# Attention scores of two pairs of heads as one block on TensorE, with the second pair's softmax a slot later

## The chip, the cores and the metric

The kernel runs on one core of a Trainium2 chip. The metric is the device time of one execution in microseconds (us). Before the change it was 1363.72 us, the median of three runs (1363.05 to 1364.31).

## The reference

One block of a streaming encoder for 256 tokens of 2048 channels, all in float32: a normalised input is projected by one wide matrix, a recurrent branch and an attention branch run side by side, sigmoid gates merge them, an output projection and an MLP of 8192 channels follow. The change lies in the attention branch alone. It has 16 heads of 64 channels, and 256 tokens are 4 chunks of 64:

```python
s = jnp.einsum('bhnqd,bhnkd->bhnqk', qc, kb) * (Dh ** -0.5) + bias[:, None]
s = jnp.where(valid[:, None, :], s, -jnp.inf)
p = jax.nn.softmax(s, axis=-1)
o = jnp.einsum('bhnqk,bhnkd->bhnqd', p, vb)
```

For each head, scores are made of queries and keys, a bias by relative distance is added, a softmax over the keys follows, and the result weighs the values.

## The kernel before, in words

**The gemms.** TensorE (PE) works without a break on large matrix products in float32 accuracy. Each piece of weights arrives by DMA (`raw_...`), ScalarE (ACT) rounds it to a high part (`wh_...`, line 91) and VectorE (DVE) subtracts to get the low part (`wl_...`, line 92); TensorE then makes three matmuls of 512 columns (lines 141 to 143: activation's high by `wh`, high by `wl`, low by `wh`). `Unit` with `run` makes 256 rows by 1024 columns in four PSUM banks (`c11`, `c12`, `c21`, `c22`, in the profile `acc_<unit>c`). Half of the inner dimension goes through seven products of blocks A, B, C, D of the weights (names such as `p21B`: bank 21, block B), the other half through plain pieces (`r0_8`: columns' half 0, inner tiles 8 and 9). A product or a piece is an item of 12 matmuls, and needs two splits of 1024 columns (a product) or one (a piece). Banks get sums and differences in between: ACT copies a bank to `u_...` (line 872), DVE subtracts it from another (line 908, called "less" below). GpSimd (POOL) issues accumulating DMAs between raw blocks (line 925).

**Slots.** `run` calls `u.step` at eleven places, the slots 0 to 10. Slot 2 lies after products 11D and 12C, and then come r1_8, slot 3, product 21A, slot 4, r1_10, slot 5, product 21B, slot 6, r0_8, slot 7, r0_10, slot 8, product 21D, slot 9, r0_12, slot 10 and the rest. Attention is cut into four pieces of work (two pairs of heads each), and each is hung on the slots of one unit: `av`, `qk`, `ga0` and `ga2`, which run one after the other.

**Attention of a pair of heads.** `attn_pair` makes the scores of two heads in one tile `s` of two PSUM banks (pool `ps_sc`, one buffer), head 0 in rows 0 to 63 and head 1 in rows 64 to 127 of the array, each in a first span of 128 columns and a second of 256 (line 694). POOL loads the bias by two DMAs of 128 KB (line 698) and masks a corner by a memset (line 699); the tile `bias` has one buffer, so that the bias of the next pair can be fetched only when the adds of this one have read it. DVE adds it (line 705, one instruction for each span, both heads in one), takes the maxima (`mx`, line 707), ACT takes the exponentials with their sums (line 710), and DVE scales by the reciprocals (`rs`, lines 712 and 714). Later slots turn the result by transposes on TensorE into the two banks of `ps_tp` (`turn`, tile `tpp`, line 720), ACT copies them out (line 722), and `attn_values` multiplies by the values (line 736), into a bank of `ps_tp` too.

**What sets the order.** Each engine runs its instructions in the order in which they stand, and an instruction whose input is late holds up all behind it. That order is made when the program is built, by a scheduler with priorities: score matmuls and weight splits are put ahead (`high_priority`), the adds and the rest of the softmax have none and are put where the scheduler holds them to be ready.

Of the kernel before, what the change touches and what calls it, by code (L numbers as in the profile page):

```python
# [8 lines left out]
F32 = mybir.dt.float32  # L9
# [3 lines left out]
ALU = mybir.AluOpType  # L13
# [3 lines left out]
P = 128  # L17
T = 256
# [4 lines left out]
NC = 512  # L23
# [27 lines left out]
def tile_hybrid_block(  # L51
# [5 lines left out]
    nc = tc.nc  # L57
# [8 lines left out]
    ps_acc, ps_tp, ps_sm = [cm.__enter__() for cm in ps_cms]  # L66
# [21 lines left out]
    casts, marks, newest, low = [], [], [], []  # L88
# [68 lines left out]
    def later(*steps):  # L157
        behind.extend([n, f] for n, f in steps)
# [109 lines left out]
    steps = [1, 1] + [2] * (KD // 2 - 1)  # L268
# [11 lines left out]
    for kt, n in zip(starts, steps):  # L280
# [6 lines left out]
        with ExitStack() as es:  # L287
# [3 lines left out]
            for j in range(n):  # L291
                g, hi = wmix[:, kt + j:kt + j + 1], xT[c][:, a + j, 0, :]
# [331 lines left out]
    def scores(n, made, gap, first=None, between=()):  # L624

        sc = []
        steps = []

        def one(i):
            if not i:  # L630
                out, fs = hgrn_scores(n, made)
                sc.extend(out)
                steps.extend(fs)
            steps[i]()

# [27 lines left out]
    s2 = scores(2, a2[0], 4)  # L663
# [3 lines left out]
    s3 = scores(3, a3[0], 4)  # L667
# [14 lines left out]
    ps_sc = ps_cms[-1].__enter__()  # L682
    yb = []
    TOK = 11

    def attn_pair(g, pr, qT, kT):

        n = g * 4 + pr
        sc = ps_sc.tile([P, 2, NC], F32, name=f"s{g}{pr}", tag="sc")
        with tc.issue_after(newest[0].ins), tc.high_priority(offset=2000):  # L690
            for d, q, k in ((slice(0, P), slice(0, P), slice(0, P)), (slice(P, 3 * P), slice(P, T), slice(0, T))):
                for j in range(2):
                    r = slice(64 * j, 64 * j + 64)
                    nc.tensor.matmul(sc[:, j, d], qT[r, q], kT[r, k], start=True, stop=True)
        bias = bp.tile([P, 2, T], F32, name=f"bias{n}", tag="bias", bufs=1)
        for j in range(2):
            rb = rel_bias[2 * n + j]
            nc.gpsimd.dma_start(bias[:, j, :], bass.AP(tensor=rb.tensor, offset=rb.offset + P + 1, ap=[[1, P], [1, T]]))
        nc.gpsimd.memset(bias[0:CH, :, 0:CH], NEG)
        s = bp.tile([P, 2, 3 * P], F32, name=f"sb{n}", tag="s", bufs=2)  # L700
        spans = (slice(0, P), slice(P, 3 * P))
        mx = small.tile([P, 2, 2], F32, name=f"mx{n}", tag="mx")
        sums = small.tile([P, 2, 2], F32, name=f"sum{n}", tag="sums")
        for d in spans:
            nc.vector.tensor_tensor(s[:, :, d], sc[:, :, d], rev(bias[:, :, 0:d.stop - d.start]), op=ALU.add)
        for b, d in enumerate(spans):
            nc.vector.tensor_reduce(mx[:, b, :], s[:, :, d], axis=AX.X, op=ALU.max, negate=True)
        for b, d in enumerate(spans):
            for j in range(2):
                nc.scalar.activation(s[:, j, d], s[:, j, d], AF.Exp, bias=mx[:, b, j:j + 1], accum_out=sums[:, b, j:j + 1])  # L710
        rs = small.tile([P, 2, 2], F32, name=f"rs{n}", tag="rs")
        nc.vector.reciprocal(rs, sums)
        for b, d in enumerate(spans):
            nc.vector.tensor_tensor(s[:, :, d], s[:, :, d], bc(rs[:, b, :], 2, d.stop - d.start), op=ALU.mult)
# [376 lines left out]
    qkT = {}  # L1091
# [37 lines left out]
    for m in range(NM):  # L1129
        scaled("k0", rstd, m, acc_k[m])  # L1130
    x_sums[3]()
    yb += [new_act(f"yb{g}") for g in range(2)]
    (p0, t0, v0), (p1, t1, v1), (p2, t2, v2), (p3, t3, v3) = chunks
    alone(Unit(lambda: xT, lambda: Sx, w_in_n, C_AV, "av", values,
               steps=at_slots((0, turn_of("k0")), (2, p0[0]), (4, p0[1]), (7, t0[0], t0[1]), (9, t0[2], t0[3])))) 

    def qk_done(m, n, acc):
        scaled("qk"[n] + "1", (rstd8, rstd)[n], m, acc)

    alone(Unit(lambda: xT, lambda: Sx, w_in_t, C_AQ + NC, "qk", qk_done, apart=HG,  # L1140
               steps=at_slots((0, v0), (1, p1[0]), (3, p1[1]), (6, t1[0], t1[1]), (9, t1[2], t1[3]))))
# [145 lines left out]
    def h_out(m, n, acc):  # L1287
        t = token(f"h1_{n}_{m}")
        with tc.high_priority(offset=2000):
# [10 lines left out]
                  steps=(lambda: h_blocks(0)) if n0 else (lambda: turned(mT, 3, "m3", ga)), start=2 if n0 else 0) for n0 in (0, 2)]  # L1300
    fin = {}
    for qd in range(NQ):
# [92 lines left out]
        for n0 in (0, 2):  # L1395
# [3 lines left out]
                              start=3 if n0 else 0, tail=last and n0 == 2, five=n0 == 2 and not last))  # L1399
# [49 lines left out]
```

## Time and profile before

| what | value |
|---|---|
| median of three runs | 1363.72 us (1363.05 to 1364.31) |
| profiled execution | 1363.58 us, of it 1361.9 us span |
| granted TensorE clock | 0.998 |
| PE busy | 1350.3 us, 99% of the span |
| DVE busy | 1166.9 us, 86% |
| ACT busy | 970.7 us, 71% |
| POOL busy | 156.3 us, 11% |
| the attention's slots | from about 250 to about 425 us of the span |

The span goes from the first to the last profiled instruction, and 1.7 us of the execution lie around it. A busy PE says that matmuls follow each other, with ends that are modelled; short waits are better seen in the starts of its instructions. In rows of a timeline the first number is the start and the second the duration, in us from the span's start; `[0.55 <-POOL bias L699]` says that the engine sat idle for 0.55 us and what ended it.

### The profile page before, as it was taken

To read this page: it belongs to the slowest core of one execution; us is meant where nothing else is said; L and a number is where in the kernel's file an instruction comes from. 1 tells how busy PE (TensorE), PEld (TensorE's weight loads), DVE (VectorE), ACT (ScalarE), POOL (GpSimd) and SP (SyncE) were. 2 spreads that over 40 slices of the span, in tenths; PEclk is the share of its full clock that TensorE was granted. 3 is DMA by queue.
4 is the path that set the end of the run, shared out by engine and by line. 5 is a ranking of instruction groups with operands and counts; after the bars stand their busy time and mean duration, and the time that the engine had idled before them with its cause. 6 is when DMAs were issued, how large, how long until landed. Compare 5 with 4: busy or idle time off the path is not lost.

```text
span 1361.9 us, 19182 instructions
## 1 busy us (share of the span) xinstructions
PE 1350.3 (99%) x6753; PEld 1116.1 (82%) x6753; DVE 1166.9 (86%) x1406; ACT 970.7 (71%) x1299; POOL 156.3 (11%) x239
## 2 busy tenths in 40 slices
PE   9999999999999999999999999999999999999997
PEld 7888888878778888888888888888888888888886
DVE  6888977887888988798998889898889988899885
ACT  6877765776777666556778767787667876678764
POOL 3000000110110000110121011100121001110210
PEclk9999999999999999999999999999999999999999
DMA  9655557778885988869898889998899988999892
GB/s 347 228 185 157 176 181 264 217 211 258 247 225 171 307 276 246 262 153 325 286 278 264 244 254 263 281 306 225 245 281 275 301 222 238 294 292 274 260 279 97
DMA packets 132498, 336.92 MB, mean 247 GB/s; under 512 B 11296, under 2 KB 14624, under 8 KB 132016
## 3 DMA queue, kind: packets, MB, share of 16 engines
q1 hardware_dynamic: 110816, 266.11, 56.4%
q0 software_dynamic: 21296, 69.28, 26.2%
q8 instruction: 53, 0.87, 0.2%
q14 instruction: 45, 0.37, 0.1%
q10 hardware_dynamic: 288, 0.29, 0.1%
HBM read 271.67 MB, written 10.49 MB: 207 GB/s over the span
## 4 chain that ended last, share of the span: by engine, by line
PE 98%; DMA 1%; ACT 0%; DVE 0%; issue 0%; SPq 0%; POOL 0%; POOLq 0%; DVEq 0%
PE acc_hq L183 2%; PE acc_hf L183 2%; PE tp_u L110 1%; PE acc_hq L188 1%; PE acc_hg L143 1%; PE acc_hi L143 1%; PE acc_hg L141 1%; PE acc_hi L142 1%; PE acc_hg L142 1%; PE acc_ga2c L141 1%; PE acc_hi L141 1%; PE acc_hf L188 1%; PE acc_ga0c L141 1%; PE acc_avc L141 1%; PE acc_dn30c L141 1%; PE acc_wo2c L143 1%
## 5 line engine op out<-in xcount | busy, mean ns | idle before, releaser
L183 PE MATMUL acc_hq<-act_x,wh_hq 128*128 128x512 f32 x128 | 41.0, 399 | 1.5 <-ACT wh_hq L91 1.2
L183 PE MATMUL acc_hf<-act_x,wh_hf 128*128 128x512 f32 x128 | 40.6, 398 | 0.4 <-DVE wh_hf L91 0.4
L1339 POOL DMA_DIRECT2D hd<-y x24 | 24.7, 1041 | 45.8 <-ACT y L1338 45.4
L188 PEld LDWEIGHTS acc_hf<-act_x,wl_hf 128*128 128x128 f32 x128 | 23.4, 188 | 5.4
L188 PEld LDWEIGHTS acc_hq<-act_x,wl_hq 128*128 128x128 f32 x128 | 23.4, 188 | 5.3 <-DVE wl_hq L92 0.2
L141 PE MATMUL acc_hg<-wh_hg,act_x 128*128 128x512 f32 x64 | 25.1, 392 | 0.0
L141 PE MATMUL acc_hi<-wh_hi,act_x 128*128 128x512 f32 x64 | 25.0, 391 | 0.0
L143 PE MATMUL acc_hg<-wh_hg,act_x 128*128 128x512 f32 x64 | 24.9, 390 | 0.0
L143 PE MATMUL acc_hi<-wh_hi,act_x 128*128 128x512 f32 x64 | 24.9, 389 | 0.0
L142 PE MATMUL acc_hi<-wl_hi,act_x 128*128 128x512 f32 x64 | 24.9, 389 | 0.0
L142 PE MATMUL acc_hg<-wl_hg,act_x 128*128 128x512 f32 x64 | 24.9, 389 | 0.0
L92 DVE TENSOR_TENSOR wl_hq<-raw_hq,wh_hq 128x1024 fp32r<-128x1024 f32 (+2 forms) x21 | 20.1, 966 | 5.4 <-ACT wh_hq L91 5.4
L188 PE MATMUL acc_hq<-act_x,wl_hq 128*128 128x256 f32 x128 | 24.6, 279 | 0.0
L188 PE MATMUL acc_hf<-act_x,wl_hf 128*128 128x256 f32 x128 | 24.6, 279 | 0.0
L92 DVE TENSOR_TENSOR wl_hf<-raw_hf,wh_hf 128x512 fp32r<-128x512 f32 (+2 forms) x26 | 20.9, 811 | 4.1 <-ACT wh_hf L91 3.9
L91 ACT CAST wh_hq<-raw_hq 128x1024 fp32r<-128x1024 f32 (+2 forms) x21 | 17.6, 842 | 8.9 <-DMA raw_hq<-in_w_in_t_dram 4.6
L92 DVE TENSOR_TENSOR act_u<-tp_u,act_u 128x512 fp32r<-128x512 f32 x28 | 19.2, 685 | 5.3 <-ACT act_u L91 5.3
L100 POOL TENSOR_TENSOR ro<-os,mhalf 128x4 f32<-128x4 f32 x4 | 4.4, 1099 | 167.4 <-DVE os L99 164.3
L92 DVE TENSOR_TENSOR wl_hg<-raw_hg,wh_hg 128x1024 fp32r<-128x1024 f32 x16 | 19.4, 1219 | 3.0 <-ACT wh_hg L91 3.0
L183 PEld LDWEIGHTS acc_hq<-act_x,wh_hq 128*128 128x128 f32 x128 | 19.9, 189 | 2.2 <-ACT wh_hq L91 1.4
L183 PEld LDWEIGHTS acc_hf<-act_x,wh_hf 128*128 128x128 f32 x128 | 19.9, 190 | 1.0 <-DVE wh_hf L91 0.7
L91 ACT CAST wh_hf<-raw_hf 128x512 fp32r<-128x512 f32 (+2 forms) x24 | 17.5, 740 | 4.4 <-PE acc_hg L143 1.6
(2295 smaller groups left out, 5327.3 us busy)
## 6 DMA issues: line engine op xcount, KB each, us to landing
raw_hi<-in_w_in_n_dram SPq DMA_DIRECT2D x16, 512.0 KB, 3.8
raw_hg<-in_w_in_n_dram SPq DMA_DIRECT2D x16, 512.0 KB, 3.7
raw_hq<-in_w_in_t_dram SPq DMA_DIRECT2D x12, 512.0 KB, 5.2
hd<-y POOLq DMA_DIRECT2D x24, 256.0 KB, 8.6
raw_hf<-in_w_in_t_dram SPq DMA_DIRECT2D x16, 256.0 KB, 5.6
raw_hf<-in_w_in_t_dram SPq DMA_DIRECT2D x8, 512.0 KB, 4.0
raw_aq<-in_w_in_t_dram SPq DMA_DIRECT2D x8, 512.0 KB, 4.4
raw_ak<-in_w_in_t_dram SPq DMA_DIRECT2D x8, 512.0 KB, 4.3
```

Source lines behind the costliest of these rows:

```text
L91: casts[:] = [(copy or nc.scalar.copy)(hi, src)]
L92: low[:] = [nc.vector.tensor_tensor(lo, src, hi.bitcast(F32), op=ALU.subtract)]
L100: nc.gpsimd.tensor_tensor(dst, ms, mhalf[:, :width], op=ALU.pow)
L110: nc.tensor.transpose(tp[:, j, :], src[:, j * P:(j + 1) * P], ident)
L141: nc.tensor.matmul(acc, hi, wh, start=first, stop=False, skip_group_check=True)
L142: nc.tensor.matmul(acc, hi, wl, start=False, stop=False, skip_group_check=True)
L143: newest[:] = [nc.tensor.matmul(acc, lo, wh, start=False, stop=last, skip_group_check=True)]
L183: newest[:] = [nc.tensor.matmul(acc[cb], wh[:, cb * P:(cb + 1) * P], r.rearrange("p u t -> p (u t)"), start=kt == 0, stop=last)]
L188: newest[:] = [nc.tensor.matmul(acc[cb][:, 0:T], wl[:, cb * P:(cb + 1) * P], r[:, 0, :], start=False, stop=False)]
L1339: nc.gpsimd.dma_start(hd[n][m], t, accum_op=ALU.add)
```

## The change

The scores of both pairs of a piece of work are made in one go, at the slot of the first pair: first the first spans of both pairs, then the second spans. The first pair's two heads get one bank each in `ps_tp`, the second pair's get the tile of `ps_sc` as before. The first pair's adds take one instruction for each head and span, four in place of two. In units `qk` and `ga2` the work moves from slots 1 and 3 to slots 2 and 4; in `av` (2 and 4) and `ga0` (3 and 5) the slots stay.

```diff
-    def attn_pair(g, pr, qT, kT):
+    SPANS = (slice(0, P), slice(P, 3 * P))
+
+    def attn_scores(g, p0, qT, kT):
+
+        first = [ps_tp.tile([P, NC], F32, name=f"s{g}{p0}{j}", tag="tp") for j in range(2)]
+        second = ps_sc.tile([P, 2, NC], F32, name=f"s{g}{p0 + 1}", tag="sc")
+        both = (first, [second[:, j, :] for j in range(2)])
+        with tc.issue_after(newest[0].ins), tc.high_priority(offset=2000):
+            for d, q, k in zip(SPANS, (slice(0, P), slice(P, T)), (slice(0, P), slice(0, T))):
+                for p in range(2):
+                    for j in range(2):
+                        r = slice(64 * j, 64 * j + 64)
+                        nc.tensor.matmul(both[p][j][:, d], qT[r, p0 + p, q], kT[r, p0 + p, k], start=True, stop=True)
+        return ([lambda d, j=j: (slice(j, j + 1), first[j][:, d].rearrange("p (j t) -> p j t", j=1)) for j in range(2)],
+                [lambda d: (slice(0, 2), second[:, :, d])])
+
+    def attn_pair(g, pr, scores):
 
         n = g * 4 + pr
-        sc = ps_sc.tile([P, 2, NC], F32, name=f"s{g}{pr}", tag="sc")
-        with tc.issue_after(newest[0].ins), tc.high_priority(offset=2000):
-            for d, q, k in ((slice(0, P), slice(0, P), slice(0, P)), (slice(P, 3 * P), slice(P, T), slice(0, T))):
-                for j in range(2):
-                    r = slice(64 * j, 64 * j + 64)
-                    nc.tensor.matmul(sc[:, j, d], qT[r, q], kT[r, k], start=True, stop=True)
...
         for d in spans:
-            nc.vector.tensor_tensor(s[:, :, d], sc[:, :, d], rev(bias[:, :, 0:d.stop - d.start]), op=ALU.add)
+            for part in scores:
+                j, sc = part(d)
+                nc.vector.tensor_tensor(s[:, j, d], sc, rev(bias[:, j, 0:d.stop - d.start]), op=ALU.add)
...
     alone(Unit(lambda: xT, lambda: Sx, w_in_n, C_AV, "av", values,
-               steps=at_slots((0, turn_of("k0")), (2, p0[0]), (4, p0[1]), (7, t0[0], t0[1]), (9, t0[2], t0[3])))) 
+               steps=at_slots((0, turn_of("k0")), (2, s0, p0[0]), (4, p0[1]), (7, t0[0], t0[1]), (9, t0[2], t0[3])))) 
...
-               steps=at_slots((0, v0), (1, p1[0]), (3, p1[1]), (6, t1[0], t1[1]), (9, t1[2], t1[3]))))
-    gate_steps = [at_slots((0, turn_of("q1"), v1), (1, turn_of("k1")), (3, p2[0]), (5, p2[1]), (7, t2[0], t2[1]), (9, t2[2], t2[3])),
-                  at_slots((0, v2), (1, p3[0]), (3, p3[1]), (6, t3[0], t3[1]), (8, t3[2], t3[3]), (10, v3))]
+               steps=at_slots((0, v0), (2, s1, p1[0]), (4, p1[1]), (6, t1[0], t1[1]), (9, t1[2], t1[3]))))
+    gate_steps = [at_slots((0, turn_of("q1"), v1), (1, turn_of("k1")), (3, s2, p2[0]), (5, p2[1]), (7, t2[0], t2[1]), (9, t2[2], t2[3])),
+                  at_slots((0, v2), (2, s3, p3[0]), (4, p3[1]), (6, t3[0], t3[1]), (8, t3[2], t3[3]), (10, v3))]
```

The built orders of POOL and of the DMA queue on SyncE are the same before and after; those of PE, DVE and ACT differ. Three places follow, where a row is an instruction with its line, what it writes and reads, and its shape (lines 705 to 925 stand 12 further down after the change).

On PE, the place of the first scores in unit `av`, before:

```order
L143 MATMUL acc_avc_2817<-wh_avp12C_2863,S_x 128x512
L694 MATMUL s_2877<-k0T,q0T 128x128 x2
L694 MATMUL s_2877<-k0T,q0T 128x256 x2
L141 MATMUL acc_avc_2817<-wh_avr_8_2901,act_x_105 128x512
L142 MATMUL acc_avc_2817<-wl_avr_8_2902,act_x_105 128x512
```

and now, with `s_2877` and `s_2878` the first pair's two banks and `s_2879` the second pair's tile:

```order
L143 MATMUL acc_avc_2817<-wh_avp12C_2863,S_x 128x512
L698 MATMUL s_2877<-k0T,q0T 128x128
L698 MATMUL s_2878<-k0T,q0T 128x128
L698 MATMUL s_2879<-k0T,q0T 128x128 x2
L698 MATMUL s_2877<-k0T,q0T 128x256
L698 MATMUL s_2878<-k0T,q0T 128x256
L698 MATMUL s_2879<-k0T,q0T 128x256 x2
L141 MATMUL acc_avc_2817<-wh_avr_8_2909,act_x_105 128x512
```

Eight score matmuls stand at one place; the four that stood between product 21A and r1_10 are gone from there.

On DVE in unit `av`, from the first pair's adds on (`sb_2886`, `bias_2882` are the first pair's, `sb_2950`, `bias_2946` the second's), before:

```order
L705 TENSOR_TENSOR sb_2886<-s_2877,bias_2882 128x2x128
L705 TENSOR_TENSOR sb_2886<-s_2877,bias_2882 128x2x256
L707 TENSOR_REDUCE mx_2887<-sb_2886 128x2 x2
L92 TENSOR_TENSOR wl_avp21B_2985<-raw_avB_2749,wh_avp21B_2984 128x1024
L92 TENSOR_TENSOR wl_avp21B_2995<-raw_avB_2751,wh_avp21B_2994 128x1024
L705 TENSOR_TENSOR sb_2950<-s_2941,bias_2946 128x2x128
L92 TENSOR_TENSOR wl_avr_8_3007<-rawp_avr_8_2765,wh_avr_8_3006 128x1024
L908 TENSOR_TENSOR acc_avc_2817<-acc_avc_2817,u_av 128x512
L712 RECIPROCAL rs_2897<-sum_2888 128x4
L705 TENSOR_TENSOR sb_2950<-s_2941,bias_2946 128x2x256
```

and now (`sb_2953`, `bias_2949` are the second pair's):

```order
L717 TENSOR_TENSOR sb_2892<-s_2878,bias_2888 128x256
L719 TENSOR_REDUCE mx_2893<-sb_2892 128x2 x2
L717 TENSOR_TENSOR sb_2953<-s_2879,bias_2949 128x2x128
L92 TENSOR_TENSOR wl_avp21B_2988<-raw_avB_2749,wh_avp21B_2987 128x1024
L92 TENSOR_TENSOR wl_avp21B_2998<-raw_avB_2751,wh_avp21B_2997 128x1024
L717 TENSOR_TENSOR sb_2953<-s_2879,bias_2949 128x2x256
L920 TENSOR_TENSOR acc_avc_2817<-acc_avc_2817,u_av 128x512
L92 TENSOR_TENSOR wl_avr_8_3010<-rawp_avr_8_2765,wh_avr_8_3009 128x1024
L724 RECIPROCAL rs_2905<-sum_2894 128x4
L92 TENSOR_TENSOR wl_avr_10_3041<-rawp_avr_10_2794,wh_avr_10_3040 128x1024
L726 TENSOR_TENSOR sb_2892<-sb_2892,rs_2905 128x2x128
```

The first add of the second pair has moved from behind the two splits for product 21B to ahead of them. Further down, the first pair's second scaling stands behind both splits for product 21D, and on PE its transposes stand four matmuls into r0_10 instead of ahead of it. DVE's order in `ga2` is now the same as in `av`; in `qk` the add stays behind the splits of 21B.

On DVE in unit `ga0`, from the second split for product 21B on, before (`sb_3752` first pair, `sb_3821` second):

```order
L92 TENSOR_TENSOR wl_ga0p21B_3847<-raw_ga0B_3576,wh_ga0p21B_3846 128x1024
L908 TENSOR_TENSOR acc_ga0c_3642<-acc_ga0c_3642,u_ga_3787 128x512
L92 TENSOR_TENSOR wl_ga0r_8_3867<-rawp_ga0r_8_3590,wh_ga0r_8_3866 128x1024
L712 RECIPROCAL rs_3763<-sum_3754 128x4
L714 TENSOR_TENSOR sb_3752<-sb_3752,rs_3763 128x2x128
L714 TENSOR_TENSOR sb_3752<-sb_3752,rs_3763 128x2x256
L92 TENSOR_TENSOR wl_ga0r_10_3898<-rawp_ga0r_10_3619,wh_ga0r_10_3897 128x1024
L705 TENSOR_TENSOR sb_3821<-s_3812,bias_3817 128x2x128
```

and now (`sb_3764` first pair, `sb_3830` second):

```order
L92 TENSOR_TENSOR wl_ga0p21B_3856<-raw_ga0B_3582,wh_ga0p21B_3855 128x1024
L717 TENSOR_TENSOR sb_3830<-s_3751,bias_3826 128x2x128
L920 TENSOR_TENSOR acc_ga0c_3648<-acc_ga0c_3648,u_ga_3801 128x512
L92 TENSOR_TENSOR wl_ga0r_8_3876<-rawp_ga0r_8_3596,wh_ga0r_8_3875 128x1024
L724 RECIPROCAL rs_3777<-sum_3766 128x4
L717 TENSOR_TENSOR sb_3830<-s_3751,bias_3826 128x2x256
L92 TENSOR_TENSOR wl_ga0r_10_3907<-rawp_ga0r_10_3625,wh_ga0r_10_3906 128x1024
L92 TENSOR_TENSOR wl_ga0p21D_3923<-rawd_ga0D_3588,wh_ga0p21D_3922 128x1024
L920 TENSOR_TENSOR acc_ga0c_3627<-acc_ga0c_3627,u_ga_3865 128x512
L92 TENSOR_TENSOR wl_ga0p21D_3933<-rawd_ga0D_3590,wh_ga0p21D_3932 128x1024
L726 TENSOR_TENSOR sb_3764<-sb_3764,rs_3777 128x2x128
L726 TENSOR_TENSOR sb_3764<-sb_3764,rs_3777 128x2x256
```

Here the second pair's first add has moved ahead of the "less" and of the splits for r0_8 and r0_10, and the first pair's scalings from ahead of the split of r0_10 to behind the splits of 21D. Its transposes on PE stand in the middle of r0_10 now, after six of its matmuls; those of the second pair stand four matmuls into r0_14, where they stood ahead of r0_12, and the scalings ahead of them stand behind the split of r1_14.

More of the change, by code (lines that the diff above doesn't have):

```diff
@@ L700, in attn_pair @@
         s = bp.tile([P, 2, 3 * P], F32, name=f"sb{n}", tag="s", bufs=2)
-        spans = (slice(0, P), slice(P, 3 * P))
+        spans = SPANS
         mx = small.tile([P, 2, 2], F32, name=f"mx{n}", tag="mx")
@@ L1108, in heads_of, with scores @@
         g, p0 = i // 2, i % 2 * 2
-        turns, pts = [], []
+        turns, pts, got = [], [], []
+        def scores():
+            got.extend(attn_scores(g, p0, qkT[f"q{g}"], qkT[f"k{g}"]))
         def pair(p):
-            qT, kT = [qkT[f"{name}{g}"][:, p0 + p, :] for name in "qk"]
-            turns.extend(attn_pair(g, p0 + p, qT, kT))
-        return ([lambda p=p: pair(p) for p in range(2)], [lambda j=j: pts.append(turns[j]()) for j in range(4)],
+            turns.extend(attn_pair(g, p0 + p, got[p]))
+        return (scores, [lambda p=p: pair(p) for p in range(2)], [lambda j=j: pts.append(turns[j]()) for j in range(4)],
                 lambda: attn_values(g, p0, (pts[:2], pts[2:]), av[g]))
@@ L1132, in tile_hybrid_block @@
     yb += [new_act(f"yb{g}") for g in range(2)]
-    (p0, t0, v0), (p1, t1, v1), (p2, t2, v2), (p3, t3, v3) = chunks
+    (s0, p0, t0, v0), (s1, p1, t1, v1), (s2, p2, t2, v2), (s3, p3, t3, v3) = chunks
     alone(Unit(lambda: xT, lambda: Sx, w_in_n, C_AV, "av", values,
-               steps=at_slots((0, turn_of("k0")), (2, p0[0]), (4, p0[1]), (7, t0[0], t0[1]), (9, t0[2], t0[3]))))
+               steps=at_slots((0, turn_of("k0")), (2, s0, p0[0]), (4, p0[1]), (7, t0[0], t0[1]), (9, t0[2], t0[3]))))
     def qk_done(m, n, acc):
```

## The prediction

> **What bounds the kernel now.** I read the page first: busy times, then the chain that ended last.
>
> ```profile
> PE 1350.3 (99%) x6753; PEld 1116.1 (82%) x6753; DVE 1166.9 (86%) x1406; ACT 970.7 (71%) x1299; POOL 156.3 (11%) x239
> PE 98%; DMA 1%; ACT 0%; DVE 0%; issue 0%; SPq 0%; POOL 0%; POOLq 0%; DVEq 0%
> ```
>
> TensorE is the bound from end to end, so whatever its queue gains or loses in the attention stretch reaches the end in full. Next the waits between 244 and 430 us (engine and line waited for: total us, times, longest).
>
> ```profile
> POOL bias L698 <- DVE mx L707: 36.9, 6, 13.4
> POOL bias L699 <- DMA bias<-in_rel_bias_dram: 32.9, 7, 5.9
> ...
> DVE sb L705 <- POOL bias L699: 6.2, 4, 2.9
> ...
> PE acc_qkc L141 <- ACT u_qk L872: 0.5, 1, 0.5
> ```
>
> TensorE waits almost nowhere (0.5 us once), but VectorE already waits 6.2 us, in four adds, for a bias that POOL has fetched. That wait costs nothing today because of what stands behind it. Is that still so after the change?
>
> **What the change saves.** TensorE's timeline around the first scores of `av`:
>
> ```profile
> 256.17 0.39 PE L143 MATMUL acc_avc<-wh_avp12C,S_x 128*128 128x512 f32 x1
> 256.49 0.93 PE L694 MATMUL s<-k0T,q0T 64*128 64x128 f32 x8
> 257.34 0.50 PE L141 MATMUL acc_avc<-wh_avr,act_x 128*128 128x512 f32 x1
> 257.68 0.39 PE L142 MATMUL acc_avc<-wl_avr,act_x 128*128 128x512 f32 x1
> ```
>
> A gemm matmul starts 0.227 us after the one before it (12 of them from 266.73 to 269.45, below). From 256.17 to 257.68 are 1.51 us, two such steps are 0.45: one block of scores costs 1.06 us. Of it 0.09 (0.32 less 0.227) is paid going in, 0.11 (0.34 less 0.227) coming out, 0.85 lies inside. A joint block pays the edges once, and that alone saves 0.20. At most it also saves what lies inside beyond the streaming: 384 columns in two passes at 0.227 us for 512 are 0.34, so 0.71. I take 0.41, near the lower middle, since part of the inside is the first weight load: a joint block costs 1.71 us, 0.65 more than one now, and the four units save 4 x 0.41 = **1.6 us** (0.8 to 2.8).
>
> The two banks of `ps_tp` cost nothing: they are free when the first pair's adds end, at about 260, and the next transposes stand at 272. The first pair's adds get longer. An add of 256 elements takes 0.42 us, one of 512 takes 0.66 (rows at 267.00 and 269.16 below), and the next starts 0.08 before the end; by that slope 128 elements take 0.30, and 2 x 0.22 + 2 x 0.34 = 1.12 us replace 0.92. These 0.2 us matter only because the bias waits for them.
>
> **What it costs, unit `av`.** VectorE's, POOL's and TensorE's timelines there:
>
> ```profile
> 258.81 1.01 DVE L705 TENSOR_TENSOR sb<-s,bias 128x256 f32<-128x256 f32 x2
> 261.66 2.46 DVE L92 TENSOR_TENSOR wl_avp21B<-raw_avB,wh_avp21B 128x1024 fp32r<-128x1024 f32 x2 [0.91 <-ACT wh_avp21B L91]
> 267.00 0.42 DVE L705 TENSOR_TENSOR sb<-s,bias 128x256 f32<-128x256 f32 x1 [2.88 <-POOL bias L699]
> 267.34 1.22 DVE L92 TENSOR_TENSOR wl_avr<-rawp_avr,wh_avr 128x1024 fp32r<-128x1024 f32 x1
> 268.48 0.69 DVE L908 TENSOR_TENSOR acc_avc<-acc_avc,u_av 128x512 f32<-128x512 f32 x1
> 269.08 0.17 DVE L712 RECIPROCAL rs<-sum 128x4 f32<-128x4 f32 x1
> 269.16 0.66 DVE L705 TENSOR_TENSOR sb<-s,bias 128x512 f32<-128x512 f32 x1
> 269.74 0.41 DVE L714 TENSOR_TENSOR sb<-sb,rs 128x256 f32<-128x256 f32 x1
> ```
> ```profile
> 260.41 1.14 POOL L698 DMA_DIRECT2D bias<-in_rel_bias_dram  x2 [8.17 <-DVE mx L707]
> 266.77 0.20 POOL L699 MEMSET bias<- 64x128 f32 x1 [5.23 <-DMA bias<-in_rel_bias_dram]
> ```
> ```profile
> 266.73 0.39 PE L141 MATMUL acc_avc<-wh_avp21B,act_x 128*128 128x512 f32 x1
> ...
> 269.45 0.39 PE L141 MATMUL acc_avc<-wh_avr,act_x 128*128 128x512 f32 x1
> ```
>
> The first adds end at 259.8; POOL issues the second pair's two bias DMAs at 260.41, masks at 266.77, and VectorE adds at 267.00. Meanwhile it had made both splits for product 21B. In the new order this add stands ahead of them, and nothing makes the bias come earlier: one buffer, the same POOL queue. So VectorE stands still until 267.2, then adds (0.34), and the first low part of 21B is there at 267.2 + 0.34 + 1.22 = 268.8. TensorE comes to 21B 0.41 earlier than now and wants that part with its second matmul, at 266.73 - 0.41 + 0.23 = 266.55: **first stall 2.2 us**.
>
> Behind it VectorE is late. From start to start a split takes 1.14 us, an add of 512 elements 0.58, a "less" 0.60, a scaling as much as an add. After the first split come the second (1.14), the add, the "less", the split for r0_8: it ends at 268.8 + 1.14 + 0.58 + 0.60 + 1.14 = 272.2. TensorE, after 11 matmuls of 21B and one of r0_8, wants it at 268.8 + 12 x 0.227 = 271.5: **second stall 0.7**. Then a reciprocal (0.09), the split for r0_10, a scaling (0.33), a split for 21D, a "less", the other split and the second scaling (0.58) take 5.0 us: the transposes can start at 277.3. TensorE is there after 11 + 4 matmuls, at 275.6: **third stall 1.7**. Sum of `av`: 4.6 us.
>
> **Unit `ga2`** has this order too; the bias comes faster.
>
> ```profile
> 398.50 1.14 POOL L698 DMA_DIRECT2D bias<-in_rel_bias_dram  x2 [6.00 <-DVE mx L707]
> 403.95 0.20 POOL L699 MEMSET bias<- 64x128 f32 x1 [4.31 <-DMA bias<-in_rel_bias_dram]
> ```
>
> From issue to memset are 5.45 us against 6.36 in `av`, so the first stall is 0.9 shorter: 1.3 + 0.7 + 1.7 = 3.7 us.
>
> **Unit `ga0`.**
>
> ```profile
> 357.92 1.14 POOL L698 DMA_DIRECT2D bias<-in_rel_bias_dram  x2 [13.45 <-DVE mx L707]
> 363.76 0.20 POOL L699 MEMSET bias<- 64x128 f32 x1 [4.71 <-DMA bias<-in_rel_bias_dram]
> ```
> ```profile
> 364.24 0.39 PE L141 MATMUL acc_ga0c<-wh_ga0r,act_x 128*128 128x512 f32 x1
> ```
> ```profile
> 368.72 1.22 DVE L92 TENSOR_TENSOR wl_ga0r<-rawp_ga0r,wh_ga0r 128x1024 fp32r<-128x1024 f32 x1
> ...
> 376.73 1.23 DVE L92 TENSOR_TENSOR wl_ga0r<-rawp_ga0r,wh_ga0r 128x1024 fp32r<-128x1024 f32 x1 [2.45 <-ACT wh_ga0r L91]
> ```
>
> Here the moved add stands ahead of the "less" and the split for r0_8. It can start at 364.0 + 0.2 = 364.2, and that split ends at 364.2 + 0.34 + 0.60 + 1.22 = 366.4; TensorE wants it at 364.24 - 0.41 + 0.23 = 364.06: 2.3 us. Reciprocal, add, split, split, "less", split and both scalings (0.2 + 0.58 + 3 x 1.14 + 0.60 + 0.91 = 5.7) end at 372.1, while TensorE is at the first pair's transposes after 11 + 6 matmuls, at 370.3: 1.8. The second pair's scalings now stand behind the split for r1_14. That split is late on a DMA: it starts 6.9 us after the end of the split for r0_12 (368.72 + 1.14 to 376.73), whose buffer it reloads. With r0_12's split at 372.1 + 1.1 it starts at 380.1, and the scalings end at 382.2. TensorE is there after the transposes (0.6) and 34 matmuls (the rest of r0_10, 21D, r0_12 and four of r0_14), at 380.4: 1.8. Sum: 5.9 us.
>
> **Unit `qk`** keeps the add behind the splits of 21B.
>
> ```profile
> 303.84 1.13 POOL L698 DMA_DIRECT2D bias<-in_rel_bias_dram  x2 [6.10 <-DVE mx L707]
> 310.90 0.20 POOL L699 MEMSET bias<- 64x128 f32 x1 [5.93 <-DMA bias<-in_rel_bias_dram]
> ```
> ```profile
> 312.65 0.39 PE L143 MATMUL acc_qkc<-wh_qkr,act_x 128*128 128x512 f32 x1
> 313.53 0.50 PE L141 MATMUL acc_qkc<-wh_qkp21B,act_x 128*128 128x512 f32 x1 [0.50 <-ACT u_qk L872]
> ...
> 316.98 0.47 PE L141 MATMUL acc_qkc<-wh_qkr,act_x 128*128 128x512 f32 x1
> ```
>
> TensorE loses 0.65 us today (0.88 less 0.227), because ACT's copy `u_qk` stands behind an exponential of the second pair. ACT's new order puts that exponential later, so this wait goes. The add, at 311.1 now (0.23 after the memset starts), comes about 2.9 us later (12 matmuls, and the longer adds), at 314.0, and the split for r0_8 ends at 316.1, about when TensorE comes (316.98 - 0.41 - 0.65 + 0.23 = 316.15). Sum: -0.65, and 0 to 1 for a later bias.
>
> **The sum.** 4.6 + 3.7 + 5.9 - 0.65 - 1.6 = 11.95: against the profiled execution (1361.9 us of span and 1.7 around it, 1363.6, as the median) **1375.6 us**. Each wait hangs on the bias's landing:
>
> ```profile
> DMA to landing us min/median/max: 3.3/5.0/6.5
> ```
>
> Of 16 these are the shortest, the middle and the longest. If the bias lands 1.5 us sooner in the three units, three times 1.5 us go: 1371. If it lands 1 us later, 3 us come: 1378.6. These are the forecast's own bounds.
>
> [...]
>
> **Rivals.** (a) Not slower: the bias lands before VectorE would miss it. From issue to memset it may then take 6.36 - 2.2 = 4.2 us in `av`, 5.45 - 1.3 = 4.1 in `ga2` and 5.84 - 2.3 = 3.5 in `ga0`. Then only the saving and the wait in `qk` count: 1363.6 - 1.6 - 0.65 = 1361.3. For it: the shortest landing, 3.3. Against: all four second biases in the rows above take 5.4 to 7.1, and it must come true three times. Chance 0.04. (b) VectorE catches up: only the first stalls count, 2.2 + 1.3 + 2.3 - 0.65 - 1.6 = 3.5, so 1367.1. For it: VectorE is only 86% busy. Against: behind the moved add its rows follow each other without a gap, and every term above is such a row. Chance 0.13. (c) `qk` stalls too, because a bias that lands as late as in its row (7.1 us from issue to memset) holds the split for r0_8 and, behind it, the transposes as in `av`: up to 0.7 + 1.7 and the wait of today not gone (0.65): 1378.7. Chance 0.13. (d) A clear gain, where the upper saving of 2.8 comes whole and no stall: 1360.1. Chance 0.02.
>
> **How the numbers follow.** The forecast has 0.68: 1375.6. No change means within 0.2% (2.7 us), about what a measurement of this kernel can tell. (a) falls there; half of (b)'s spread lies close to its edge, so same has 0.05, faster 0.02, slower 0.93. The range takes the forecast's own bounds and (c), and leaves 1 us below for a larger saving by the joint blocks: 1370 to 1379.
>
> **What would show it.** In the profile after: waits of DVE `sb` for POOL `bias` of about 6 us in `av`, 4 in `ga0`, 5 in `ga2`, in place of 6.2 in all; on TensorE new gaps in front of `wl_avp21B`, `wl_ga0r`, `wl_ga2p21B` and of three or four groups of `tpp`; four blocks of scores, 1.7 us each; no wait for `u_qk`. Wrong would be an add that waits long while TensorE does not, or score blocks that save more than 0.7 each.

## The result, and the profile after

The changed kernel takes 1377.56 us, the median of five runs (1374.08 to 1381.33), against 1364.14 (1363.05 to 1364.65) for the kernel before beside it: a ratio of 1.0101, with a 95% interval of 1.0079 to 1.0123. Four runs on another occasion gave 1376.53 and 1.0094 (1.0078 to 1.0111). The forecast was 1375.6. The profiled execution took 1379.65 us, of it 1378.0 span.

Busy times and the chain that ended last, from the page:

```profile
PE 1356.0 (98%) x6753; PEld 1120.0 (81%) x6753; DVE 1168.3 (85%) x1414; ACT 971.2 (70%) x1299; POOL 156.3 (11%) x239
PE 89%; DMA 3%; DVE 3%; ACT 2%; issue 2%; POOL 0%; SPq 0%; POOLq 0%; ACTq 0%; DVEq 0%
```

VectorE's, ScalarE's and GpSimd's busy times are as before; TensorE is on 89% of the chain instead of 98%, so most of the new time is waiting (its busy time grew by 5.7 us, in part by a slower clock, told below). The waits between 244 and 446 us (engine and line waited for: total us, times, longest):

```profile
POOL bias L709 <- DMA bias<-in_rel_bias_dram: 35.7, 7, 6.5
DVE sb L717 <- POOL bias L709: 14.5, 4, 6.0
...
PE tpp L732 <- DVE sb L726: 6.0, 4, 2.6
...
PE acc_avc L142 <- DVE wl_avp21B L92: 1.8, 1, 1.8
...
PE acc_ga2c L142 <- DVE wl_ga2p21B L92: 0.7, 1, 0.7
...
PE acc_ga0c L142 <- DVE wl_ga0p22A L92: 0.4, 1, 0.4
```

VectorE waits 14.5 us for the bias in four adds, where it waited 6.2, and TensorE now waits for VectorE's splits and for its scalings (line 726, ahead of the transposes). The wait for `u_qk` is gone. VectorE's and then TensorE's timeline in `av`:

```profile
260.49 1.00 DVE L719 TENSOR_REDUCE mx<-sb 128x2 f32<-128x256 f32 x2
267.49 0.42 DVE L717 TENSOR_TENSOR sb<-s,bias 128x256 f32<-128x256 f32 x1 [6.00 <-POOL bias L709]
267.84 2.35 DVE L92 TENSOR_TENSOR wl_avp21B<-raw_avB,wh_avp21B 128x1024 fp32r<-128x1024 f32 x2
...
276.84 0.69 DVE L726 TENSOR_TENSOR sb<-sb,rs 128x512 f32<-128x512 f32 x1
```
```profile
256.79 0.39 PE L143 MATMUL acc_avc<-wh_avp12C,S_x 128*128 128x512 f32 x1
257.10 1.58 PE L698 MATMUL s<-k0T,q0T 64*128 64x128 f32 x16
258.61 0.50 PE L141 MATMUL acc_avc<-wh_avr,act_x 128*128 128x512 f32 x1
258.95 0.40 PE L142 MATMUL acc_avc<-wl_avr,act_x 128*128 128x512 f32 x1
...
269.11 0.50 PE L142 MATMUL acc_avc<-wl_avp21B,act_x 128*128 128x512 f32 x1 [1.81 <-DVE wl_avp21B L92]
...
277.67 0.85 PE L732 MATMUL tpp<-ident,sb 128*128 128x128 f32 x6 [0.52 <-DVE sb L726]
```

The second pair's add stands at the head of VectorE's queue and stops it for 6.00 us; both splits for 21B start only behind it, and TensorE stands still for 1.81 us. The joint block itself goes from 256.79 to 258.95: 2.16 us less two steps of 0.227 is 1.71, the forecast's figure; it is so in all four units.

How much later each unit's first matmul comes than in the profile before, taken as differences from unit to unit (us gained or lost inside the unit), beside the forecast and the experiments that follow:

| profile | `av` | `qk` | `ga0` | `ga2` | sum |
|---|---|---|---|---|---|
| forecast (stalls less 0.41 a block) | +4.2 | -1.06 | +5.5 | +3.3 | +11.95 |
| changed kernel | +3.88 | -1.07 | +7.41 | +2.91 | +13.1 |
| changed kernel, second profile | +3.89 | -1.05 | +8.19 | +3.06 | +14.1 |
| changed, two bias tiles | -0.55 | -1.26 | +0.47 | -0.43 | -1.8 |
| before, two bias tiles | -0.11 | -0.83 | +0.08 | -0.04 | -0.9 |
| changed, adds behind r0_8 | +1.13 | -1.26 | +3.86 | +0.79 | +4.5 |
| before, order alone | +3.49 | +0.18 | +3.81 | +0.31 | +7.8 |
| two tiles, `ga0` on slots 2 and 4 | -0.55 | -1.27 | -0.36 | -0.47 | -2.7 |
| joint block in `qk` alone | -0.12 | -1.05 | +0.86 | -0.04 | -0.4 |
| before, gaps made behind the attention | -0.13 | -0.79 | 0.00 | -0.05 | -1.0 |

The last row's kernel has the attention of the kernel before, instruction for instruction; its -0.79 in `qk` is what two executions of the same work can differ by (told with the run that made the gaps). What lies outside these units differs by up to 0.6 us at the start and at the end from one execution to the next; the first profile of the changed kernel has 2.5 us more at two waits near 1250 us, in the MLP.

### The profile page after: what moved, and what is told of

The parts are those of the page before. It is cut to its first block, busy times and chain, and to the rows that moved or that the text cites. A ratio compares the mean times of both kernels' runs of the same rounds, so it can differ in the third digit from the quotient of the medians.

```text
span 1378.0 us, 19190 instructions
## 1 busy us (share of the span) xinstructions
PE 1356.0 (98%) x6753; PEld 1120.0 (81%) x6753; DVE 1168.3 (85%) x1414; ACT 971.2 (70%) x1299; POOL 156.3 (11%) x239
## 4 chain that ended last, share of the span: by engine, by line
PE 89%; DMA 3%; DVE 3%; ACT 2%; issue 2%; POOL 0%; SPq 0%; POOLq 0%; ACTq 0%; DVEq 0%
PE acc_hf L183 2%; PE acc_hq L183 2%; PE acc_hf L188 1%; PE acc_hq L188 1%; PE acc_hg L141 1%; PE acc_hi L141 1%; PE acc_hi L142 1%; PE acc_hg L143 1%; PE acc_hg L142 1%; PE acc_hi L143 1%; PE acc_dn30c L141 1%; PE acc_wo2c L143 1%; PE acc_dn00c L143 1%; PE acc_up00c L143 1%; PE acc_dn20c L143 1%
## 5 line engine op out<-in xcount | busy, mean ns | idle before, releaser
L722 ACT ACTIVATE sb<-sb,mx 128x128 f32<-128x128 f32 (+1 forms) x32 | 14.3, 448 | 12.3 <-DVE mx L719 12.3
```

## The experiments

Theory W is the prediction's: the loss is VectorE standing at the second pair's add until its bias has landed. Theory J, its rival: the joint block itself costs (more adds, eight score matmuls in a row, the transposes' banks taken early).

**Take the wait away.** The second pair's bias gets a tile of its own, without more memory: the four transposed-weight buffers become two of twice the size, and one of them is idle when the bias is needed (the remark behind `#` is not in the code).

```diff
-        bias = bp.tile([P, 2, T], F32, name=f"bias{n}", tag="bias", bufs=1)
+        if pr % 2:
+            bias = bp.tile([P, 2, 3 * P], F32, name=f"bias{n}", tag="pt", bufs=2)[:, :, 0:T]
+        else:
+            bias = bp.tile([P, 2, T], F32, name=f"bias{n}", tag="bias", bufs=1)
...
-            pt = bp.tile([P, 3, P], F32, name=f"pt{n}{j}", tag="pt", bufs=4)
+            pt = both[0][:, j]     # both: one tile of tag "pt", bufs=2, for the pair
```

> The changed kernel, but the second pair's bias gets a tile of its own (a buffer of the softmax's transposed weights that is idle then), so POOL can fetch it without waiting for the first pair's adds. Nothing else is changed. Theory W (the loss is the second pair's add standing at the head of VectorE's queue while its bias lands): the waits of VectorE for the bias fall from 14.5 us to under 2, TensorE's gaps of 1.97 and 0.68 us in av, 0.34, 1.67 and 2.78 in ga0, 0.8, 0.6 and 1.6 in ga2 go, and so does the half clock behind two of them. What is left is the saving by the joint blocks (1.6) and the wait for u_qk that is gone (0.65): 1363.6 - 2.25 = 1361.3, in the range 1360 to 1364. Theory J (the joint block itself costs: four adds for two, eight score matmuls in a row, the transposes' banks taken earlier): the time stays above 1370 although the bias is early.

Measured: 1362.45 us (11 runs) against 1363.43 (21 runs), ratio 0.9992 (0.9983 to 1.0001). VectorE's order in `av` still has the second pair's adds ahead of both splits, but nothing waits there, and the one wait for the bias left in the stretch is short; what TensorE has is one wait in `ga0`. VectorE's timeline in `av`, and the waits:

```profile
259.49 1.00 DVE L722 TENSOR_REDUCE mx<-sb 128x2 f32<-128x256 f32 x2
260.41 1.01 DVE L720 TENSOR_TENSOR sb<-s,bias 128x256 f32<-128x256 f32 x2
261.34 1.00 DVE L722 TENSOR_REDUCE mx<-sb 128x2 f32<-128x256 f32 x2
262.26 2.35 DVE L92 TENSOR_TENSOR wl_avp21B<-raw_avB,wh_avp21B 128x1024 fp32r<-128x1024 f32 x2
```
```profile
DVE sb L720 <- POOL bias L712: 0.9, 1, 0.9
...
PE acc_ga0c L141 <- ACT u_ga L891: 0.4, 1, 0.4
```

The 15 us between this kernel and the changed one went with the wait, while the joint blocks stayed. Theory J falls: it asked for more than 1370. The gain is smaller than the 2.25 us expected, and the profile has ScalarE's copy `u_ga` late in `ga0`; a later run takes that wait away.

**The same tile in the kernel before.**

> The kernel before with the same second tile for the bias, its score blocks apart as they were. Theory W: in the kernel before the 6.2 us of waits for the bias stood behind the splits and held up nothing but the 0.5 us for u_qk, so the time is 1363 to 1364, and the changed kernel with two tiles is 1.6 to 2.3 us below this one. If the early bias is by itself worth something, this one gains as much as the changed kernel does with it, and the joint blocks are worth nothing.

Measured: 1363.69 us (11 runs) against 1363.43, ratio 1.0002 (0.9993 to 1.0010). The early bias is worth nothing measurable by itself. In its profile the wait for `u_qk` is missing (-0.83 in `qk`), but so it is in the table's last row (-0.79), where the bias has one tile; the gain can't be put down to the second tile. Between the two kernels with two tiles lie 1.24 us. By their profiles it is four blocks at 1.71 against eight at 1.06, 4 x 0.40 = 1.6, less the new wait in `ga0`, about 0.8.

**Move the adds, keep one tile.** The second pair's softmax is hung on slot 7, and its adds are held behind the split of r0_8.

```diff
+        behind = lows[-1].ins
...
-                nc.vector.tensor_tensor(s[:, j, d], sc, rev(bias[:, j, 0:d.stop - d.start]), op=ALU.add)
+                with ExitStack() as es:
+                    if pr % 2:
+                        es.enter_context(tc.issue_after(behind))
+                    nc.vector.tensor_tensor(s[:, j, d], sc, rev(bias[:, j, 0:d.stop - d.start]), op=ALU.add)
```

> The changed kernel with one bias tile as it is; the second pair's softmax is hung on slot 7 and its adds are held behind the split of r0_8, so they no longer stand ahead of the splits for 21B and r0_8. Joint score blocks, banks and adds as in the changed kernel. Theory W: VectorE's waits for the bias fall below 5 us and the gaps ahead of 21B and r0_8 go (in av 2.0, in ga0 0.3, in ga2 0.8 and 0.6 us, and behind them the first transposes' 0.7, 1.7 and 1.6), while the second pair's softmax is later by a split or two and its transposes may wait, the 2.8 us of ga0 most of all: 1367, in the range 1363 to 1371. Theory J: 1375 or more, as the changed kernel.

Measured: 1369.01 us (1366.79 to 1369.59), ratio 1.0039 (1.0025 to 1.0053). The one large wait left in the stretch:

```profile
PE tpp L736 <- DVE sb L730: 5.1, 3, 2.5
```

No add waits for the bias any more, and no gap stands ahead of 21B or r0_8. What stays is the second pair's transposes, since its softmax is now late: 5.6 us of loss are left of some 13, with one bias tile and the same joint blocks (its profile has 1352.4 us of busy TensorE and a mean granted clock of 0.997, where the two-tile version has 1348.7 and 0.998, so a slower clock may be part of them). W's figure held; J's did not.

**The order without the change.** In the kernel before, the first split for product 21B is held behind the second pair's first add. No joint block anywhere.

```diff
+                    if not g and (i, name) == ("21", "B") and second_add:
+                        es.enter_context(tc.issue_after(second_add.pop().ins))
                     wh, wl = parts(raw, f"{self.what}p{i}{name}{g}")
```

> The kernel before with one edit: the first split for product 21B is held behind the second pair's first add, in all four units. Score blocks apart, one bias tile, two adds a pair: no joint block anywhere. Theory W: the same loss comes without the change: a gap of about 2 us ahead of the low part of 21B in av (the add at 267.0 in the kernel before, then 0.34 + 1.22 for the split: 268.6, wanted at 266.96), 0 to 2 in the others, and waits of the transposes behind: 1368 to 1376. Theory J: no joint block, no loss: 1363 to 1365.

Measured: 1371.13 us (1370.49 to 1372.81), ratio 1.0059 (1.0045 to 1.0073). VectorE and TensorE in `av`:

```profile
266.76 0.42 DVE L706 TENSOR_TENSOR sb<-s,bias 128x256 f32<-128x256 f32 x1 [6.13 <-POOL bias L700]
267.10 1.22 DVE L92 TENSOR_TENSOR wl_avp21B<-raw_avB,wh_avp21B 128x1024 fp32r<-128x1024 f32 x1
```
```profile
268.37 0.50 PE L142 MATMUL acc_avc<-wl_avp21B,act_x 128*128 128x512 f32 x1 [1.38 <-DVE wl_avp21B L92]
```

The unit loses 3.49 us in `av`, where the changed kernel with its blocks' saving of 0.41 loses 3.88. In `ga2` it loses almost nothing: there the second pair's bias is asked for earlier (the kernel before has that unit's attention on slots 1 and 3), and the add waits only 1.60 us. So the order, with one bias tile, is enough for a loss, as far as the bias is late. The sum is 7.8 us and not 13: in `ga0` this edit puts the add ahead of another split than the change does, so the units can be compared one by one in `av` alone.

**Where the last 0.8 us of the two-tile version went.** Two tiles, and the attention of `ga0` on slots 2 and 4 instead of 3 and 5:

```diff
-    ... (3, s2, p2[0]), (5, p2[1]), (7, t2[0], t2[1]), ...
+    ... (2, s2, p2[0]), (4, p2[1]), (7, t2[0], t2[1]), ...
```

> The changed kernel with two bias tiles (as in the run that gave 1362.45 us), and in ga0 the attention hung on slots 2 and 4 in place of 3 and 5. In that run TensorE waited in ga0 for ACT's copy u_ga (its queue 0.79 us behind the kernel before with two tiles at that point), half of what the four joint blocks had saved. Theory W with the blocks' saving of 0.40 each: that wait goes, so 0.8 us less, 1361.7, range 1360.8 to 1362.6, and 1.3 to 2.3 us below the kernel before. If the copy is late whatever the slot, it stays at 1362.4.

Measured: 1360.96 us (11 runs) against 1363.34 (21 runs), ratio 0.9983 (0.9974 to 0.9992). The wait for `u_ga` is gone, `ga0` gains 0.36 instead of losing 0.47, and TensorE is on 99% of the chain. This version is faster than both kernels. By the profiles 0.8 of the 1.5 us between the two medians is this wait; where the rest comes from is not shown.

**The joint block in `qk` alone.** The other units make each pair's scores at its own slot again (a function `pair_scores` with the four matmuls of the kernel before), with one bias tile.

> The changed kernel with the joint block in unit qk alone (slots 2 and 4 there); in av, ga0 and ga2 each pair's scores are made at its own slot again, as before the change. One bias tile. By the prediction's steps qk loses nothing and gains the wait for u_qk (0.65) and one block's saving (0.4): 1362.4 where the kernel before has 1363.4, range 1361.8 to 1363.4; a gain under 0.2% that the runs may not tell from none. In the changed kernel's trace qk also had a wait of 0.18 ahead of r0_8 and 0.6 to 1.2 behind, at the start of ga0; if those are the price of qk's new order, this run shows no gain: 1363.4 to 1364.

Measured: 1362.82 us (11 runs) against 1363.34, ratio 0.9999 (0.9990 to 1.0008): no difference that can be told. Inside `qk` the gain against the profile before is 1.05 as the prediction had it (0.26 against the table's last row), but `ga0` behind it loses 0.86. TensorE there:

```profile
348.04 0.66 PE L110 MATMUL tp_k<-ident,k 128*128 128x128 f32 x4 [0.22 <-DVE act_yb L92]
```

VectorE's last split of `qk` comes 1.15 us later than in the kernel before, though TensorE is 0.7 us earlier; here and, below, before:

```profile
330.45 1.22 DVE L92 TENSOR_TENSOR wl_qkr<-rawp_qkr,wh_qkr 128x1024 fp32r<-128x1024 f32 x1 [2.67 <-ACT wh_qkr L91]
```
```profile
329.30 1.23 DVE L92 TENSOR_TENSOR wl_qkr<-rawp_qkr,wh_qkr 128x1024 fp32r<-128x1024 f32 x1 [2.89 <-ACT wh_qkr L91]
```

That the later softmax of `qk` pushes it is likely, but was not tried by itself; in the two versions with an early bias, joint block in `qk` included, `ga0` loses under 0.1 us there. The changed kernel has such waits too (`wl_ga0p22A` in its list of waits, and `tp_k`): 1.2 us by the starts in its first profile and 0.2 in its second.

**The clock.** In the first profile of the changed kernel matmuls behind two gaps start 0.427 us apart instead of 0.227. TensorE stood still at 267.29 to 269.11 and at 383.29 to 385.91. The windows below start or end where the granted clock changed; columns are the window and its length, busy time of PE, PEld, DVE, ACT and POOL (with the number of instructions), the granted clock, and the DMA engines' busy share and GB/s:

```profile
266.40:269.81 3.41, 1.60 (x7) 1.01 (x7) 2.32 (x3) 1.18 (x3) 0.20 (x1) 1.00 0.02 6
269.81:273.22 3.41, 3.41 (x10) 2.63 (x9) 3.41 (x6) 1.04 (x1) 1.07 (x2) 0.50 0.70 225
273.22:276.64 3.42, 3.42 (x16) 2.79 (x16) 3.42 (x5) 1.90 (x3) 0.00 (x0) 1.00 0.86 183
382.45:385.86 3.41, 0.84 (x4) 0.38 (x2) 2.26 (x4) 1.99 (x2) 0.00 (x0) 1.00 0.53 179
385.86:389.28 3.42, 3.37 (x11) 2.99 (x12) 2.26 (x2) 2.27 (x4) 0.56 (x1) 0.50 0.48 153
389.28:392.69 3.41, 3.41 (x16) 2.78 (x15) 0.81 (x1) 2.28 (x3) 0.32 (x1) 1.00 0.77 154
```

The two stretches at 0.50 last 3.41 and 3.42 us, and their starts, 269.81 and 385.86, lie 34 times 3.413 us apart.

To see what sets this off, the kernel before got gaps in places that have nothing to do with the attention (the remark behind `#` is not in the code):

```diff
             lows.append(split(dst[0], dst[1], src))
+            for _ in range(repeats(what)):     # 3 to 6 at product 21B's first split in the later units
+                lows[-1] = nc.vector.tensor_tensor(dst[1], src, dst[0].bitcast(F32), op=ALU.subtract)
```

> The kernel before, untouched in the attention; in the output projection and the MLP the first split for each product 21B is made 3 to 6 times in a row (the same values), so that TensorE stands still there for different times, up to some 4 us, at many places. Nothing else changes. It is to tell what makes the clock drop to 0.50 behind a gap. Theory P (windows of 3.4 us that run on by themselves, a window mostly idle is followed by one at half clock): each drop lasts 3.4 us, the drops' starts are a whole number of 3.41 us apart, and gaps of the same length around 2 us are followed by a drop or not by where they lie. Theory L (length alone): every gap over some length near 2 us is followed by a drop, and none under it. Theory B (both drops came of the attention's work or of its DMAs): no drop here at all.

Measured: 1461.32 us in a single run, with a mean granted clock of 0.976 where the runs of the kernel before have 0.997 to 0.999. Its profile has 16 gaps of 1.75 to 6.84 us, and 12 drops to 0.50, four of 3.41 us and eight of 6.83: 68.3 us together, where 0.976 over the span of 1459.6 us comes to 70. Two gaps of nearly the same length, 2.09 us (955.43 to 957.52) and 1.78 us (1002.24 to 1004.02), in windows of 3.41 us (999.69 lies 12 times 3.413 us behind 958.73, where the clock changed):

```profile
955.32:958.73 3.41, 1.32 (x6) 1.04 (x6) 3.41 (x4) 0.79 (x1) 0.00 (x0) 1.00 0.29 103
958.73:962.15 3.42, 3.42 (x9) 2.66 (x9) 2.80 (x4) 0.49 (x1) 0.00 (x0) 0.50 0.90 265
962.15:965.56 3.41, 3.41 (x16) 2.65 (x15) 2.58 (x3) 2.61 (x4) 0.00 (x0) 1.00 0.65 223
999.69:1003.10 3.41, 2.55 (x12) 1.78 (x10) 3.41 (x5) 2.00 (x3) 0.00 (x0) 1.00 0.86 299
1003.10:1006.52 3.42, 1.89 (x7) 1.28 (x8) 3.42 (x4) 0.00 (x0) 0.00 (x0) 1.00 0.61 220
1006.52:1009.93 3.41, 3.41 (x16) 2.63 (x15) 0.85 (x1) 0.98 (x1) 0.00 (x0) 1.00 0.72 223
```

The window with 2.09 us of idle TensorE is followed by 0.50; the two that share the other gap, with 0.86 and 1.53 us idle, are followed by 1.00. The rows agree with theory P on where a gap lies, but eight of the 12 drops last twice the 3.4 us that it asks for; that drops start a whole number of 3.41 us apart is shown above for the two of the changed kernel, and by no row here. B, the attention as cause, falls: none runs at 955 us. Theory L asks for a length; the next run settles it.

The same profile shows something on `qk` that was not asked of it. Its attention is that of the kernel before, yet TensorE does not wait for `u_qk` ahead of 21B, where the profile before has 0.50 us of idle:

```profile
303.95 1.12 POOL L709 DMA_DIRECT2D bias<-in_rel_bias_dram  x2 [6.61 <-DVE mx L718]
310.15 0.20 POOL L710 MEMSET bias<- 64x128 f32 x1 [5.08 <-DMA bias<-in_rel_bias_dram]
```
```profile
313.00 0.40 PE L141 MATMUL acc_qkc<-wh_qkp21B,act_x 128*128 128x512 f32 x1
```

From issue to memset the bias took 6.20 us here and 7.06 there, and the exponential ahead of the copy came 0.75 us sooner. So the wait for `u_qk` comes and goes with a landing, from one execution to the next.

**The changed kernel again.**

> The changed kernel as it is, a second profiled execution of it, to tell what in the first one was the kernel's and what was chance. Theory W: the same adds wait for the same biases and the gaps come at the same places; each gap's size goes with its bias's landing, so ga0's gap ahead of r0_8 (0.34 in the first profile, 2.3 by the prediction) may be anything from 0 to 2. Theory P (half clock for 3.41 us behind a window of 3.41 us with at least 1.8 us idle): the drops behind av's and ga0's gaps may come or not, by where the windows lie, 1.7 us each; so the times of this kernel spread over 3 to 6 us and the granted clock is lower in the longer ones. The waits near 1250 us (0.4 and 1.5 us), which lie outside the attention, are not the kernel's and do not come again. Otherwise: if the drops are the work's own, they come at the same two places whatever the windows do.

Measured: 1376.53 us (1375.07 to 1378.90), ratio 1.0094 (1.0078 to 1.0111). The gap ahead of 21B in `av` has the same length, 1.82 us, but it lies across two windows, and no drop follows. The windows of both gaps; behind the one in `ga0` the clock drops:

```profile
264.30:267.72 3.42, 2.07 (x10) 1.37 (x8) 1.14 (x2) 2.36 (x4) 0.20 (x1) 1.00 0.21 83
267.72:271.13 3.41, 2.94 (x12) 2.17 (x12) 3.41 (x5) 1.16 (x2) 0.70 (x2) 1.00 0.46 149
271.13:274.54 3.41, 2.96 (x14) 2.38 (x14) 3.41 (x6) 1.48 (x3) 0.37 (x1) 1.00 0.78 203
380.36:383.77 3.41, 1.07 (x5) 0.56 (x3) 1.47 (x2) 1.99 (x2) 0.00 (x0) 1.00 0.61 213
383.77:387.18 3.41, 2.58 (x9) 2.34 (x10) 3.05 (x4) 1.49 (x3) 0.00 (x0) 0.50 0.46 157
387.18:390.60 3.42, 3.42 (x9) 2.64 (x8) 0.00 (x0) 2.48 (x4) 0.89 (x1) 0.50 0.58 115
390.60:394.01 3.41, 3.41 (x16) 2.82 (x15) 2.48 (x3) 1.65 (x2) 0.00 (x0) 1.00 0.20 38
```

So length alone does not tell these two gaps apart (L falls): 1.81 us was followed by 3.41 us at 0.50 in the first profile, 1.82 us by none here. What differs in the rows is how much of the idle time lies in one window, 1.81 us there, 1.35 and 0.47 here. The waits near 1250 us did not come again, as expected. The expectation that the longer runs have the lower clock did not hold: 1378.90 us had 0.998, 1375.07 had 0.996. The mean clock also counts time behind the last gemms of an execution (in the profile before, 1358.00 to 1361.90 us, with no matmul, had 0.50), so it doesn't tell these drops apart, and the runs' spread of 4 to 7 us is not explained by them alone.

## Why the prediction was right

**The mechanism** was shown from three sides: take the wait away and keep the rest (1362.45), move the adds out of the way (1369.01), or bring the order without the change (1371.13). The profile has the signs that were named: the wait for the bias in `av` (6.00), four blocks of 1.7, the gaps ahead of 21B, r0_8 and the transposes, and none for `u_qk`. One sign was off: the wait in `ga0`, named as 4 us, was 1.63.

**The saving.** 1.71 for a joint block was exact: 0.40 each, 1.6 in all.

**`av`** (4.2 forecast, 3.9 twice). In the second profile the three stalls are there, 1.82, 0.45 and 1.40 us of idle; by the starts of TensorE's instructions they cost 2.1, 0.7 and 1.6 where 2.2, 0.7 and 1.7 had been worked out. In the first the second one is missing and the third is down to 0.52 of idle, since the half clock behind the first slowed TensorE by 1.6 us while VectorE caught up; the unit lost the same 3.9. The slower clock cost nothing here, where the engine would have had to wait anyway.

**`qk`** (-1.06, measured -1.07 and -1.05). The new order does take the wait for `u_qk` away, with a bias that takes 7.02 us from issue to memset. That the wait was there to be gained is luck of the one profile before: against the same attention with a faster bias (-0.79 in the table) the gain is 0.27, less than the block's saving. The term "0 to 1 for a later bias" was looked for at r0_8, where 0.18 is lost; more is paid at the start of `ga0` (1.2 and 0.2 us), which the sum did not have.

**`ga2`** (3.3, measured 2.9 and 3.1): by the starts 0.9, 0.7 and 1.5 us in the first profile for 1.3, 0.7 and 1.7. Its bias took 4.95 us from issue to memset instead of 5.45, which is the first stall's difference.

**`ga0`** (5.5, measured 7.4 and 8.2) was mis-sized. The first stall, 2.3, rested on a bias that takes 5.84 us from issue to memset, as before. It took 3.88 (3.95 in the second profile). POOL's and VectorE's timelines, with TensorE's last transposes:

```profile
362.68 1.13 POOL L708 DMA_DIRECT2D bias<-in_rel_bias_dram  x2 [13.05 <-DVE mx L719]
366.56 0.20 POOL L709 MEMSET bias<- 64x128 f32 x1 [2.75 <-DMA bias<-in_rel_bias_dram]
```
```profile
374.47 1.22 DVE L92 TENSOR_TENSOR wl_ga0r<-rawp_ga0r,wh_ga0r 128x1024 fp32r<-128x1024 f32 x1
...
383.60 1.22 DVE L92 TENSOR_TENSOR wl_ga0r<-rawp_ga0r,wh_ga0r 128x1024 fp32r<-128x1024 f32 x1 [2.48 <-ACT wh_ga0r L91]
384.74 1.02 DVE L726 TENSOR_TENSOR sb<-sb,rs 128x256 f32<-128x256 f32 x2
```
```profile
385.91 1.51 PE L732 MATMUL tpp<-ident,sb 128*128 128x128 f32 x6 [2.61 <-DVE sb L726]
```

So the first stall cost 0.45 us by the starts of TensorE's instructions (0.53 in the second profile), and the first transposes 1.7, as forecast (1.8). The second transposes cost 2.8 us (3.2 in the second profile) where 1.8 was forecast. They hang on the split for r1_14 (383.60), and that hangs on a load that SyncE issues as soon as VectorE's split for r0_12 has read the buffer: 375.71, where that split ends at 374.47 + 1.22. SyncE's issue and the cast that waits for the load, after the change and, below, before:

```profile
375.71 0.37 SPq L216 DMA_DIRECT2D rawp_ga0r<-in_w_in_t_dram  x1
382.52 1.05 ACT L91 CAST wh_ga0r<-rawp_ga0r 128x1024 fp32r<-128x1024 f32 x1 [2.26 <-DMA rawp_ga0r<-in_w_in_t_dram]
```
```profile
369.97 0.37 SPq L216 DMA_DIRECT2D rawp_ga0r<-in_w_in_t_dram  x1
375.65 1.05 ACT L91 CAST wh_ga0r<-rawp_ga0r 128x1024 fp32r<-128x1024 f32 x1 [2.62 <-DMA rawp_ga0r<-in_w_in_t_dram]
```

From issue to cast 6.81 us passed (7.37 in the second profile) instead of 5.68, and the forecast's 6.9 between the two splits became 8.0 and 8.5. That is about what the third stall came out longer. So this load took 5.68, 6.81 and 7.37 us from issue to cast in three profiles; why it is slow in one and fast in another is open. The three stalls together made 4.9 and 5.4 against 5.9.

Two terms were in no step of the prediction: the half clock behind that long gap, 1.7 us (3.41 us at half speed) in the first profile and 3.0 (6.83 us, of which 0.84 idle) in the second, and the start of the unit, 1.2 and 0.2. With the block's saving the first profile's terms make 1.2 + 4.9 + 1.7 - 0.4 = 7.4 of 7.41, the second's 0.2 + 5.4 + 3.0 - 0.4 = 8.2 of 8.19. The total came out 1 to 2 us above the forecast and inside its range by luck, in so far as the two missing terms and the shorter first stall nearly cancel.

**The rivals.** (a) gave 1361.3 for a bias that lands in time, and the two-tile kernel, where that was brought about, has 1362.45; in the two profiles of the changed kernel landings went from 3.2 to 7.5 us. In `ga0` the bias came nearly as soon as (a) asks (3.88 for 3.5), and the first stall nearly went. (b) falls with the transposes' waits. (c) falls: `qk`'s bias did land late (7.02), but its split for r0_8 costs 0.18. (d) falls with the stalls.

## What to carry to other kernels

An instruction that waits on a single-buffered tile must not stand ahead of work that the bound engine needs soon (here 6.00 us of VectorE's waiting made 1.81 us of idle TensorE in `av`): look for what is queued behind it, and give the tile a second buffer, here one that lay idle, before work is merged so that its consumers become ready earlier. A term that hangs on a transfer is as uncertain as the transfer: here the same load took 5.7 to 7.4 us and the same bias 6.2 or 7.1, so a wait seen in one profile should be looked for in a second before it is counted as a gain. A change that saves 1.6 us on TensorE cost 1% with the wait; with a second tile and `ga0` on earlier slots the kernel was 0.17% faster.

## What the hardware showed that had not been expected

TensorE's granted clock was 0.50 behind some gaps of 1.81 to 3.17 us: in the changed kernel, and in a kernel whose gaps have nothing to do with the attention. The rows above, of three profiles, show eight windows at full clock together with the next one: the four with 1.81, 2.09, 2.34 and 2.57 us of idle TensorE, of 3.41, were followed by one at 0.50, the four with 0.47, 0.86, 1.35 and 1.53 us by one at full clock. Of the five windows at 0.50 the one with 0.84 us idle was followed by another, the four with 0.05 or less by full clock. A gap of 1.81 us was thus followed by 3.41 us at 0.50 in one profile, and one of 1.82 us by none in the other. What decides it beyond these rows was not shown.
